# A two-layer decoder trunk on one core: the mixer's fourteen input columns in another order

## The chip, the cores and the metric

The kernel runs on one core of one Trainium2 chip. The metric is the device time of one execution in microseconds (us). A core has five engines with queues of their own: TensorE (PE), VectorE (DVE), ScalarE (ACT), GpSimd (POOL), and SyncE (SP), which here issues most of the DMAs. Each engine works off its own queue in order; the engines wait for each other through semaphores.

## The reference

The input x has 512 positions of 1024 values, in 32-bit floats. Two layers do three residual steps each, of which the middle one is the mixer:

```python
for l in range(DEPTH):                      # DEPTH = 2
    x = x + 0.5 * swiglu(rms_norm(x, norm_ffn1[l]), ffn1...[l])
    h = rms_norm(x, norm_mix[l])
    proj = h @ w_in[l]                      # the columns of three groups of heads
    p_rwkv = token_shift(proj[..., :D_SHIFT], shift_mu[l])   # r, k, v, low rank
    y_rwkv = rwkv7_mixer(p_rwkv, ...)       # 6 heads of 64
    y_attn = dilated_attention(q, k, v)     # 6 heads, three patterns of blocks of 128
    y_conv = conv_mixer(u, ...)             # 256 channels
    x = x + concat(y_rwkv, y_attn, y_conv) @ w_out[l]
    x = x + 0.5 * swiglu(rms_norm(x, norm_ffn2[l]), ffn2...[l])
```

The convolution group takes two halves of its columns, `z = u1 * sigmoid(u2)`, convolves each channel with 31 taps along the positions, normalizes over the 256 channels and applies SiLU. The RWKV group mixes each projected column with that of the position before (token shift), makes decays and rates from the low-rank columns, and runs a recurrence over the positions.

## The kernel before

**Tiling.** x is kept transposed, as eight tiles of 128 channels by 512 positions. Each product of 32-bit floats is made of three matmuls of rounded parts (`mm3`, L124 to L126: high part by high part, high by low, low by high). A weight of 128 x 1024 comes by a DMA of SP into a buffer `raw`; ScalarE copies its high part `hi` (L113) and VectorE makes the low part `lo` (L118); for some of them ScalarE and an adding DMA make it instead (L115, L116). Three buffers of each are turned over; a generator `feed` issues the weights of a stage ahead of their use. PSUM has four banks of tag g, two of b and two of c.

**The norm.** The square sums over the channels are gathered on VectorE while x is finished. `norm_sum` (L201) adds them over the partitions with four small matmuls and takes the root, `norm_spread` (L208) spreads the result over all partitions with four more (L196) and copies it to the tile R. The projected columns are multiplied by R after the matmuls.

**The mixer's columns.** The generator `columns` (L358) makes 14 columns of `w_in`, each of 8 x 3 matmuls, and gives control back after each three. The order of the columns in it is also written into the list of weights (L342). In before it makes the gate and the value of the first convolution pair (12, 10), then the low-rank column (9), three of k (3, 4, 5), three of r (0, 1, 2), three of v (6, 7, 8), and the second convolution pair (13, 11). `finish` (L402) multiplies a column by R and does the token shift; `conv_gate` (L977) makes z of a pair.

**The RWKV preparation.** Between pieces of the columns the program places the preparation for three groups of two heads: `first` (low-rank matmuls, decays, scans), `second` (L478: r into the tile AR), `scores` (L484: matmuls of BK and AR at L491, then copies to XM and masked copies to GG at L497), `fourth` (BF on GpSimd), `third` (the products of v; transposes at L536), `fifth` (transposes at L549). `step(n)` sets n pieces of columns in between, and `need` runs the columns until the named one is there. `inverses` (L565) sends the scores XM through DRAM (dX) into a tile Ei of 96 blocks of 32 x 32, inverts them with 60 operations of VectorE (L584, L590) through a buffer tm, copies the transpose (L593), and sends both back to DRAM, from where `load` brings them as EB.

**The convolution's taps.** `taps` (L994) sets a sum to the last tap on ScalarE and adds the other 30 with one operation of VectorE each (L1007), on 482 to 511 positions. They have a low priority, so that the scheduler may set other work ahead of them, and they may be bound to stand behind a given instruction (`after`). In before, those of the first pair are bound behind `second(2)`, those of the second pair behind the copy that ends the inverse.

**Behind the columns.** The generator `filler` makes the attention's projection (L873 to L875, each output on a PSUM bank of tag g), its scores, weights and values (`att_core`, L907), and the end of the convolution (`conv`, L1012: the mean over the channels by two matmuls at L1017, one for each pair; the squares and their sums at L1026; the spread at L196; the normalized result `chi`, `clo`). The recurrence of eight steps (p3, p4, s1 to s4, L637 to L707) is placed in between by numbers of steps. The product with `w_out` starts with the convolution's results, as soon as they are there.

**What sets the order.** Within an engine, the order follows the order of the program and the priorities; a scheduler writes the queues when the kernel is built. Buffers of the same name are shared: `conv_gate` of the first pair uses the buffers x7 (as "cu") and x6 (as "cw"), and tm in the inverse also uses x7, as do some temporaries of the preparation.

Of the kernel before, what the change touches and what calls it, by code (L numbers as in the profile page):

```python
# [40 lines left out]
NP = 3  # L41
# [41 lines left out]
class Kern:  # L83
# [213 lines left out]
    def mixer(self, l):  # L297
        nc, tc, I = self.nc, self.tc, self.I
# [4 lines left out]
        def pa(n, j=0, w=1):  # L303
            o = l * NPAR + PAR[n] + j
            return self.par[:, o : o + w]

        mx = ctx.enter_context(tc.tile_pool(name=self.n("mix"), bufs=1))
        mt = lambda j, sh, nm, dt=F32: mx.tile(sh, dt, tag=f"m{j}", name=self.n(nm))
# [24 lines left out]
        L = m1.tile([P, T], F32, name=self.n("L"))  # L333
# [5 lines left out]
        pp = tc.tile_pool(name=self.n("prep"), bufs=1)  # L339
        pr = pp.__enter__()  # L340

        srcs = [(I["win"][l, c], 1024) for c in (12, 10, 9, 3, 4, 5, 0, 1, 2, 6, 7, 8, 13, 11)]  # L342
        srcs += [(I["watt"][l, w, kp], 2 * H * HD) for w in (1, 0, 2) for kp in range(4)]
        wo = lambda j, a, b: (I["wout"][l, j, :, a * P : b * P], (b - a) * P)
        srcs += [wo(j, 0, 2) for j in range(NH)] + [wo(j, 2, 5) for j in range(NH)]
# [3 lines left out]
        def column(ps):  # L349
            hi, lo = next(self.fd)  # L350
            for k in range(KT):
                s = slice(k * P, (k + 1) * P)
                self.mm3(ps, hi[:, s], lo[:, s], self.xh[k], self.xl[k], k == 0, k == KT - 1)
                yield 1
# [2 lines left out]

        def columns():  # L358

            pss = [self.psum() for _ in range(2)]  # L360
            for ps in pss:
                yield from column(ps)
            self.norm_sum()
            ps = self.psum()
            yield from column(ps)
            self.norm_spread()
            self.conv_gate(0, mt, pss, zp)
            finish(9, L, ps)
            lora_in()
            for n, q in [("k", q) for q in range(NP)] + [("r", q) for q in range(NP)] + [("v", q) for q in range(NP)]:  # L370
                ps = self.psum()
                yield from column(ps)
                if n == "k":
                    finish(3 + q, ks[q], ps)
                elif n == "r":
                    ks[q] = self.xt(q, "r")
                    finish(q, ks[q], ps)
                else:
                    vs[q] = self.xt((3, 5, 4)[q], "vv")
                    finish(6 + q, vs[q], ps)  # L380
                done.add((n, q))
            pss = [self.psum() for _ in range(2)]
            for ps in pss:
                yield from column(ps)
            self.conv_gate(1, mt, pss, zp)

        def step(n):
            for _ in range(n):
# [2 lines left out]
        def need(*a):  # L391
            while a not in done:
                next(work)

        zp, acc, vs, kns = [], [], [None] * NP, {}
        def lora_in():

            A.activation(L[0:32], L[0:32], AF.Tanh)
            A.activation(L[64:128], L[64:128], AF.Tanh, scale=0.5)
            V.tensor_scalar(L[64:128], L[64:128], 0.5, 0.5, op0=ALU.mult, op1=ALU.add)  # L400

        def finish(c, out, ps):  # L402
            raw = pr.tile([P, T + 1], F32, tag="sraw", name=self.n("sraw"), bufs=2)
            G.memset(raw[:, 0:1], 0.0)
            V.tensor_tensor(raw[:, 1:], ps, self.R, op=ALU.mult)
            t = self.nrm.tile([P, T], F32, tag=("acc", "sq")[c % 2], name=self.n("st"))
            A.activation(t, raw[:, 0:T], AF.Copy, scale=pa("mu", c))
            V.scalar_tensor_tensor(out, raw[:, 1:], der[:, c : c + 1], t, op0=ALU.mult, op1=ALU.add)
# [69 lines left out]
        def second(q):  # L478
            AR, BK, Pm = Q[q]
            need("r", q)  # L480
            r = ks[q]
            return V.tensor_tensor(AR[:, :, 1], v3(r), Pm[:, :, 1:], op=ALU.mult)

        def scores(q):  # L484

            AR, BK = Q[q][:2]
            for c0 in range(0, NC, 4):
                pss = [self.psum("b", 2).rearrange("p (c x t) -> p c x t", c=4, x=2) for _ in range(2)]
                for c in range(4):
                    for h in range(2):  # L490
                        mm(pss[h][:, c], lhsT=BK[half[h], c0 + c, h : h + 2], rhs=AR[half[h], c0 + c], start=True, stop=True)  # L491
                    if c % 2 == 1:
                        step(PS[4])
                for h in range(2):
                    r, o = half[h], half[1 - h]
                    A.copy(XM[r, c0 : c0 + 4, q], pss[h][r])
                    V.tensor_tensor(  # L497
                        GG[q][o, c0 : c0 + 4, h],
                        pss[h][o],
                        mask[o].unsqueeze(1).broadcast_to([HD, 4, 2, HD]),  # L500
                        op=ALU.mult,
                    )

            G.tensor_tensor(
                XM[:, :, q, 0], XM[:, :, q, 0], mask[:, 0].unsqueeze(1).broadcast_to([P, NC, HD]), op=ALU.mult
            )
# [35 lines left out]
        def fifth(q):  # L542

            BF = Q[q]
            for c0 in range(0, NC, 4):
                ps = self.psum("b", 2)
                n = min(4, NC - 1 - c0)
                for c in range(n):
                    nc.tensor.transpose(ps[:, c * P : (c + 1) * P], BF[:, c0 + c].rearrange("p x t -> p (x t)"), ident)  # L549
                A.copy(NKB[:, c0 : c0 + n, q], ps.rearrange("p (c h t) -> p c h t", c=4, h=2)[:, 0:n])  # L550
# [58 lines left out]

        att = at = EB = conv = bp = None  # L610
        work = columns()
        first(0)
        first(1)
# [4 lines left out]
        second(1)  # L618
        scores(1)
        fifth(0)  # L620
        self.taps(0, zp, acc, mt, pa, second(2))
        scores(2)
        after = inverses()
        fourth(1)
# [139 lines left out]
        for c in range(NC):  # L764
            n = c + 1 < NC
# [372 lines left out]
```

## Time and profile before

| | |
|---|---|
| median of 3 runs | 2071.22 us (2067.39 to 2073.70) |
| profiled execution | 2071.77 us |
| its span, first to last instruction | 2069.9 us |
| granted TensorE clock, mean | 0.990 |
| read from HBM | 183.47 MB, 93 GB/s over the span |

One execution was recorded instruction by instruction. A row of the timeline gives the start in us, the duration, the engine, the line, the operation with output and inputs, how many followed each other, and in brackets how long the engine waited before and for whom. A row of the waits gives the waiting engine, tile and line, for whom it waited, then the sum in us, how many, and the mean. A row of the windows gives the stretch, then for PE, PEld (TensorE's weight loads), DVE, ACT and POOL the busy time and count, the granted clock, the DMA engines' share, and their GB/s; where only TensorE is asked for it holds PE alone. A row of a group gives least/median/greatest duration in ns.

### The profile page before, as it was taken

The page shows a single profiled execution, that of the slowest core. Times are in us where ns is not written, and L with a number is a line of the kernel's source. Part 1 is how long each engine was busy: PE and PEld are TensorE (multiplying, and loading weights), DVE is VectorE, ACT ScalarE, POOL GpSimd, SP SyncE. Part 2 cuts the span into 40 slices and gives each one's busy share as a digit, 9 for nine tenths or more (in the row PEclk, how much of TensorE's full clock was granted, in tenths as well). Part 3 has the DMA queues.
Part 4 walks back from the last instruction along what each step waited for, and adds up shares of the span by engine and source line. Part 5 has one row for each costly group of instructions (what it writes and reads, how often), then busy time and mean ns, then how long its engine had stood idle before and what let it go on. Part 6 is the DMA issues. An engine that isn't in the chain of part 4 may idle for free.

```text
span 2069.9 us, 26110 instructions
## 1 busy us (share of the span) xinstructions
PE 2028.1 (98%) x10406; PEld 1652.0 (80%) x10406; DVE 1087.2 (53%) x1539; ACT 770.6 (37%) x1162; POOL 346.4 (17%) x324
## 2 busy tenths in 40 slices
PE   8999999989999999999999999999899999999999
PEld 6888888768877888888888888887687678888887
DVE  5545433389866555443335454324898764554422
ACT  4323222563365432323233232226634653323221
POOL 3101101232411311110111111002323112111100
PEclk9999999989999999999999999999999999999999
DMA  4332334443312433333333333334423134323332
GB/s 169 92 102 92 97 110 124 122 110 87 86 58 72 141 97 93 101 94 98 95 101 92 100 94 97 116 116 124 115 80 105 38 104 119 100 92 102 99 110 66
DMA packets 85609, 207.44 MB, mean 100 GB/s; under 512 B 27056, under 2 KB 32688, under 8 KB 85488
## 3 DMA queue, kind: packets, MB, share of 16 engines
q1 hardware_dynamic: 81312, 191.79, 30.7%
q0 software_dynamic: 3744, 13.63, 3.4%
q8 instruction: 81, 1.33, 0.3%
q10 hardware_dynamic: 432, 0.36, 0.1%
q14 instruction: 40, 0.33, 0.0%
HBM read 183.47 MB, written 8.65 MB: 93 GB/s over the span
## 4 chain that ended last, share of the span: by engine, by line
PE 86%; DVE 8%; ACT 3%; issue 2%; DMA 1%; POOL 1%; SPq 0%; ACTq 0%; POOLq 0%; DVEq 0%
PE psg L124 25%; PE psg L126 25%; PE psg L125 25%; DVE cacc L1007 2%; DVE lo L118 1%; PE psg L921 1%; PE psb L491 1%; PE psc L956 1%; DVE xl L178 1%; PE psg L875 1%; DVE Ei L590 1%; PE psg L873 1%; DMA lo<-raw 1%; DVE tm L584 1%; PE psg L874 1%
## 5 line engine op out<-in xcount | busy, mean ns | idle before, releaser
L113 ACT CAST hi<-raw 128x1024 fp32r<-128x1024 f32 (+3 forms) x368 | 350.8, 953 | 965.2 <-PE psg L125 826.9
L124 PE MATMUL psg<-xh,hi 128*128 128x512 f32 x1632 | 644.2, 395 | 7.1 <-ACT xh L177 7.1
L126 PE MATMUL psg<-xh,lo 128*128 128x512 f32 x1632 | 641.8, 393 | 1.8 <-DMA lo<-raw 1.7
L125 PE MATMUL psg<-xl,hi 128*128 128x512 f32 x1632 | 640.2, 392 | 0.2
L118 DVE TENSOR_TENSOR lo<-raw,hi 128x1024 fp32r<-128x1024 f32 (+4 forms) x342 | 461.3, 1349 | 336.3 <-ACT hi L113 326.9
L124 PEld LDWEIGHTS psg<-xh,hi 128*128 128x128 f32 x1632 | 309.0, 189 | 74.5 <-ACT xh L177 7.1
L126 PEld LDWEIGHTS psg<-xh,lo 128*128 128x128 f32 x1632 | 308.8, 189 | 68.1 <-DMA lo<-raw 2.9
L125 PEld LDWEIGHTS psg<-xl,hi 128*128 128x128 f32 x1632 | 309.0, 189 | 67.3 <-DVE xl L178 2.9
L124 PE MATMUL psg<-ah,hi 128*128 128x512 f32 x704 | 273.9, 389 | 0.0
L125 PE MATMUL psg<-al,hi 128*128 128x512 f32 x704 | 273.9, 389 | 0.0
L126 PE MATMUL psg<-ah,lo 128*128 128x512 f32 x704 | 273.9, 389 | 0.0
L224 POOL TENSOR_TENSOR s<-s,u 128x512 f32<-128x512 f32 x88 | 121.3, 1378 | 801.6 <-ACT hi L113 704.6
L223 DVE TENSOR_TENSOR u<-psg,R 128x512 f32<-128x512 f32 x88 | 60.8, 691 | 265.2 <-PE psg L126 264.9
L126 PEld LDWEIGHTS psg<-ah,lo 128*128 128x128 f32 x704 | 132.2, 188 | 27.5
L125 PEld LDWEIGHTS psg<-al,hi 128*128 128x128 f32 x704 | 132.2, 188 | 27.4
L124 PEld LDWEIGHTS psg<-ah,hi 128*128 128x128 f32 x704 | 132.2, 188 | 27.3
L221 DVE TENSOR_TENSOR g<-psg,R 128x512 f32<-128x512 f32 x88 | 60.8, 691 | 124.6 <-PE psg L126 124.6
L186 POOL TENSOR_TENSOR acc<-acc,sq 128x512 f32<-128x512 f32 x42 | 59.1, 1408 | 377.0 <-ACT sq L185 376.4
L1007 DVE SCALAR_TENSOR_TENSOR cacc<-z,par,cacc 128x482 f32<-128x482 f32 (+14 forms) x120 | 104.6, 872 | 1.7
L129 ACT CAST ah<-s 128x512 fp32r<-128x512 f32 x88 | 54.9, 623 | 122.2 <-POOL s L224 122.2
L130 DVE TENSOR_TENSOR al<-s,ah 128x512 fp32r<-128x512 f32 x88 | 59.8, 680 | 22.8 <-ACT ah L129 22.8
L873 PE MATMUL psg<-hi,xh 128*128 128x384 f32 x192 | 65.8, 346 | 4.7 <-ACT nat L898 4.7
(210 smaller groups left out, 1855.8 us busy)
## 6 DMA issues: line engine op xcount, KB each, us to landing
raw<-in_wgu_dram SPq DMA_DIRECT2D x176, 512.0 KB, 3.5
raw<-in_wd_dram SPq DMA_DIRECT2D x64, 512.0 KB, 3.5
raw<-in_win_dram SPq DMA_DIRECT2D x28, 512.0 KB, 3.6
lo<-raw POOLq DMA_DIRECT2D x26, 512.0 KB, 4.6
raw<-in_wd_dram SPq DMA_DIRECT2D x32, 384.0 KB, 3.2
raw<-in_watt_dram SPq DMA_DIRECT2D x24, 384.0 KB, 3.1
raw<-in_wout_dram SPq DMA_DIRECT2D x28, 192.0 KB, 2.3
xs<-x SPq DMA_DIRECT2D x16, 256.0 KB, 2.0
```

The costliest lines, as they stand in the source:

```text
L113: nc.scalar.copy(hi[:, :cols], raw[:, :cols])
L118: nc.vector.tensor_tensor(lo[:, :cols], raw[:, :cols], hi[:, :cols].bitcast(F32), op=ALU.subtract)
L124: mm(out, lhsT=whi, rhs=xhi, start=first, stop=False)
L125: mm(out, lhsT=whi, rhs=xlo, start=False, stop=False)
L126: mm(out, lhsT=wlo, rhs=xhi, start=False, stop=last)
L130: self.nc.vector.tensor_tensor(lo, src, hi.bitcast(F32), op=ALU.subtract)
L186: nc.gpsimd.tensor_tensor(self.acc, self.acc, sq, op=ALU.add)
L221: nc.vector.tensor_tensor(t[0], p[0], self.R, op=ALU.mult)
L223: nc.vector.tensor_tensor(t[1], p[1], self.R, op=ALU.mult)
L224: nc.gpsimd.tensor_tensor(t[2], t[2], t[1], op=ALU.mult)
L873: mm(o, lhsT=self.xh[kk][:, t], rhs=hi[:, s], start=kk == 0, stop=False)
L1007: nc.vector.scalar_tensor_tensor(a[:, d:], z[:, 0 : T - d], pa("dww", u * CW + j), a[:, d:], op0=ALU.mult, op1=ALU.add)
```

## The change

The columns come in the order low-rank, three of k, three of r, first convolution pair, three of v, second convolution pair. The norm's sums (`norm_sum`) stand behind the first column, which is now the low-rank one; the spread, the low-rank column's finish and its activations stand behind the second one (the first of k). The taps of the first pair are called right behind its gate, inside the generator, and are no longer bound to another instruction; they keep their low priority. Nothing is computed otherwise, and the number of matmuls is the same.

```diff
-        srcs = [(I["win"][l, c], 1024) for c in (12, 10, 9, 3, 4, 5, 0, 1, 2, 6, 7, 8, 13, 11)]
+        srcs = [(I["win"][l, c], 1024) for c in (9, 3, 4, 5, 0, 1, 2, 12, 10, 6, 7, 8, 13, 11)]
...
         def columns():
 
-            pss = [self.psum() for _ in range(2)]
-            for ps in pss:
-                yield from column(ps)
+            low = self.psum()
+            yield from column(low)
             self.norm_sum()
-            ps = self.psum()
-            yield from column(ps)
-            self.norm_spread()
-            self.conv_gate(0, mt, pss, zp)
-            finish(9, L, ps)
-            lora_in()
-            for n, q in [("k", q) for q in range(NP)] + [("r", q) for q in range(NP)] + [("v", q) for q in range(NP)]:
+            for n, q in [(n, q) for n in "krcv" for q in range(NP) if n != "c" or q == 0] + [("c", 1)]:
+                if n == "c":
+                    pss = [self.psum() for _ in range(2)]
+                    for ps in pss:
+                        yield from column(ps)
+                    self.conv_gate(q, mt, pss, zp)
+                    if q == 0:
+                        self.taps(0, zp, acc, mt, pa, None)
+                    continue
                 ps = self.psum()
                 yield from column(ps)
+                if (n, q) == ("k", 0):
+                    self.norm_spread()
+                    finish(9, L, low)
+                    lora_in()
                 if n == "k":
                     finish(3 + q, ks[q], ps)
...
                 done.add((n, q))
-            pss = [self.psum() for _ in range(2)]
-            for ps in pss:
-                yield from column(ps)
-            self.conv_gate(1, mt, pss, zp)
...
         fifth(0)
-        self.taps(0, zp, acc, mt, pa, second(2))
+        second(2)
         scores(2)
```

The changed kernel's lines from here on have a number greater by one than before (the taps are at L1008, GG at L498, the mean at L1018).

VectorE's queue around the scores of group 2 in layer 0, before (GG_2568 and GG_2569 are the masked scores of groups 1 and 2, cacc the sum of the first convolution pair, sraw the first v column):

```order
L482 TENSOR_TENSOR AR_3037<-r_3173,Pm_3070 128x8x64
L497 TENSOR_TENSOR GG_2568<-psb_3139,tab 64x4x128
L510 SCALAR_TENSOR_TENSOR r_3173<-r_3173,par,kn_3109 128x512
L1007 SCALAR_TENSOR_TENSOR cacc_3192<-z_2719,par,cacc_3192 128x482
L1007 SCALAR_TENSOR_TENSOR cacc_3192<-z_2719,par,cacc_3192 128x483
L1007 SCALAR_TENSOR_TENSOR cacc_3192<-z_2719,par,cacc_3192 128x484
L1007 SCALAR_TENSOR_TENSOR cacc_3192<-z_2719,par,cacc_3192 128x485
L497 TENSOR_TENSOR GG_2569<-psb_3224,tab 64x4x128
L497 TENSOR_TENSOR GG_2569<-psb_3225,tab 64x4x128
L405 TENSOR_TENSOR sraw_3354<-psg_3180,R_2712 128x512
```

The same place in the changed kernel:

```order
L483 TENSOR_TENSOR AR_2966<-r_3102,Pm_2999 128x8x64
L498 TENSOR_TENSOR GG_2568<-psb_3068,tab 64x4x128
L511 SCALAR_TENSOR_TENSOR r_3102<-r_3102,par,kn_3038 128x512
L498 TENSOR_TENSOR GG_2569<-psb_3122,tab 64x4x128
L498 TENSOR_TENSOR GG_2569<-psb_3123,tab 64x4x128
L498 TENSOR_TENSOR GG_2569<-psb_3142,tab 64x4x128
L498 TENSOR_TENSOR GG_2569<-psb_3143,tab 64x4x128
L991 SCALAR_TENSOR_TENSOR cw_3283<-psg_3110,R_2680 128x512
L406 TENSOR_TENSOR sraw_3354<-psg_3321,R_2680 128x512
```

The four taps between the scores of groups 1 and 2 are gone; a part of the first pair's gate (cw) now stands between GG and the v column.

VectorE's queue at the end of the inverse in layer 0, before (Et is the transposed inverse, lo a weight of the attention's projection, cacc_3589 the second pair's sum):

```order
L584 TENSOR_TENSOR tm_3272<-Ei_3269 96x30
L590 TENSOR_TENSOR Ei_3269<-Ei_3269,tm_3272 96x30
L593 COPY Et_3270<-Ei_3269 96x1024
L1007 SCALAR_TENSOR_TENSOR cacc_3589<-z_3563,par,cacc_3589 128x482
L118 TENSOR_TENSOR lo_4012<-raw_4010,hi_4011 128x768
L1007 SCALAR_TENSOR_TENSOR cacc_3589<-z_3563,par,cacc_3589 128x483
```

There in the changed kernel (cu, cw and z_3287 are of the first pair, cuw and z_3563 of the second):

```order
L585 TENSOR_TENSOR tm_3170<-Ei_3167 96x30
L591 TENSOR_TENSOR Ei_3167<-Ei_3167,tm_3170 96x30
L594 COPY Et_3168<-Ei_3167 96x1024
L989 TENSOR_TENSOR cu_3282<-psg_3109,R_2680 128x512
L993 SCALAR_TENSOR_TENSOR z_3287<-cu_3282,cw_3283 128x512
L993 SCALAR_TENSOR_TENSOR z_3563<-cuw_3559 128x512
L118 TENSOR_TENSOR lo_3687<-raw_3685,hi_3686 128x768
L1008 SCALAR_TENSOR_TENSOR cacc_3289<-z_3287,par,cacc_3289 128x482
L1008 SCALAR_TENSOR_TENSOR cacc_3589<-z_3563,par,cacc_3589 128x482
```

Both gates end behind the inverse, and the taps of both pairs follow it in turn, where before only those of the second pair did.

TensorE's queue around the convolution's mean in layer 0, before (EB, Z, A and E, SVU belong to the recurrence; pT, vt, pe and qkT to the attention):

```order
L947 MATMUL psg_4602<-tab,pe_4498 128x128 x4
L1017 MATMUL psg_4626<-cacc_3192,onesm 128x512
L1017 MATMUL psg_4626<-cacc_3589,onesm 128x512
L641 MATMUL psb_4608<-EB_3570,XM_2570 64x64 x6
L678 MATMUL psb_4617<-A_802_4589,E_785_4516 64x64 x6
L956 MATMUL psc_4631<-pT_4536,vt_3754 64x128 x2
L956 MATMUL psc_4631<-pT_4601,vt_3754 64x128 x3
L650 MATMUL psb_4634<-EB_3570,Z_4615 64x64 x6
L701 MATMUL psc_4591<-SVU_2572,XM_2570 64x64
L1026 MATMUL psg_4660<-onesm,z_2719 128x1
```

In the changed kernel, around the second of the two matmuls of the mean (the first stands 29 rows ahead):

```order
L660 MATMUL psb_4884<-SVU_2572,GG_2569 64x64 x2
L679 MATMUL psb_4918<-A_870_4891,E_853_4803 64x64 x6
L1018 MATMUL psg_4626<-cacc_3589,onesm 128x512
L667 MATMUL psc_4893<-SVU_2572,GG_2567 64x64 x2
L667 MATMUL psc_4893<-SVU_2572,GG_2568 64x64 x2
L667 MATMUL psc_4893<-SVU_2572,GG_2569 64x64 x2
L702 MATMUL psc_4893<-SVU_2572,XM_2570 64x64
L1027 MATMUL psg_4660<-onesm,z_3287 128x1
L922 MATMUL psg_4673<-qkT_3972,qkT_4338 128x512
```

The second matmul of the mean and the sums of the squares now stand behind the products at L679 of the recurrence's last step; behind them only the last step's products at L667 and L702 are left of the recurrence.

## The prediction

> **What bounds the kernel now.** I read the page's busy times first, then the busy time and clock by stage, the list of what TensorE waited for, the timelines around its longest waits, and the clock in stretches of 4 us.
>
> ```profile
> span 2069.9 us, 26110 instructions
> PE 2028.1 (98%) x10406; PEld 1652.0 (80%) x10406; DVE 1087.2 (53%) x1539; ACT 770.6 (37%) x1162; POOL 346.4 (17%) x324
> ```
>
> TensorE (PE) is busy for 98% of the span. Its matmuls stay the same in number and kind, so the change can only move idle time (42 us in all) and time at a low clock. The next rows cut the mixer of layer 0 at the first column, the first attention matmul, and the first W_out matmul; then the first two stages in layer 1.
>
> ```profile
> 372.40:496.60 124.20, 114.49 (x549) 89.53 (x548) 86.52 (x135) 75.28 (x108) 37.32 (x41) 0.93 0.47 115
> 496.60:602.90 106.30, 102.62 (x975) 85.99 (x973) 87.34 (x203) 47.06 (x104) 34.73 (x37) 0.97 0.29 79
> 602.90:720.00 117.10, 114.82 (x669) 86.45 (x668) 71.15 (x150) 62.59 (x129) 24.69 (x25) 1.00 0.34 97
> ...
> 1401.40:1525.60 124.20, 114.47 (x559) 89.81 (x558) 87.82 (x138) 76.11 (x108) 37.20 (x41) 0.95 0.47 115
> 1525.60:1630.00 104.40, 101.25 (x986) 84.83 (x984) 87.38 (x207) 47.78 (x106) 35.19 (x38) 0.98 0.29 81
> ```
>
> The columns' stage loses 9.7 us of idle time in each layer and 7% and 5% of the clock; the second stage loses 3.7 and 3.2 us of idle time. TensorE's waits over the whole program:
>
> ```profile
> PE psb L491 <- DVE GG L497: 10.6, 4, 4.8
> ...
> PE psb L536 <- DVE vv L408: 5.0, 2, 2.5
> PE psg L873 <- ACT nat L898: 4.7, 6, 1.8
> ...
> PE psb L549 <- ACT SVU L540: 0.4, 2, 0.2
> ```
>
> Two long waits per layer, for GG and for vv, are most of it. TensorE, VectorE and GpSimd there, in layer 0:
>
> ```profile
> 428.75 1.87 PE L491 MATMUL psb<-AR,BK 64*128 64x128 f32 x16 [0.48 <-DVE GG L497]
> ...
> 460.90 2.79 PE L491 MATMUL psb<-AR,BK 64*128 64x128 f32 x16 [4.80 <-DVE GG L497]
> ...
> 479.14 0.66 PE L536 MATMUL psb<-tab,vv 128*128 128x128 f32 x4 [2.48 <-DVE vv L408]
> ```
> ```profile
> 453.06 7.06 DVE L1007 SCALAR_TENSOR_TENSOR cacc<-z,par,cacc 128x482 f32<-128x482 f32 x4
> 460.15 1.41 DVE L497 TENSOR_TENSOR GG<-psb,tab 64x512 f32<-64x512 f32 x2
> ```
> ```profile
> 454.23 4.61 POOL L514 TENSOR_TENSOR BF<-BK,fd 64x1024 f32<-64x1024 f32 x2
> ```
>
> Four taps of the convolution stand in VectorE's queue ahead of GG and take 7.06 us, while GpSimd works on BF; GG starts as they end, and TensorE right after. The wait for vv has the same origin. The clock, in stretches of 4 us (TensorE's busy time, instructions, granted clock):
>
> ```profile
> 436.00:440.00 4.00, 4.00 (x11) 0.50 0.41 130
> ...
> 460.00:464.00 4.00, 3.10 (x17) 0.50 0.66 131
> 464.00:468.00 4.00, 4.00 (x13) 0.75 0.28 49
> ...
> 480.00:484.00 4.00, 4.00 (x16) 0.61 0.62 197
> ...
> 592.00:596.00 4.00, 4.00 (x14) 0.54 0.00 0
> ```
> ```profile
> 1488.00:1492.00 4.00, 3.30 (x17) 0.50 0.68 135
> 1492.00:1496.00 4.00, 4.00 (x17) 0.82 0.33 57
> ...
> 1508.00:1512.00 4.00, 4.00 (x18) 0.69 0.66 197
> ```
>
> Half the clock follows both long waits, and comes twice (436 and 592) in stretches of small matmuls without a long wait.
>
> **The columns' stage.** The changed order has no tap ahead of GG and vv, so 4.80 + 2.48 + 0.2 = **7.5 us** of waiting go in each layer. With them go the two drops of the clock behind: busy time by missing clock is 3.10 x 0.50 + 4.00 x 0.25 + 4.00 x 0.39 = 4.1 in layer 0 and 3.30 x 0.50 + 4.00 x 0.18 + 4.00 x 0.31 = 3.6 in layer 1. The drop at 436 stays, since the scores and low-rank matmuls before it stand as close as before.
>
> What comes in: the same preparation meets fewer column matmuls as cover. A column matmul is issued every 0.227 us:
>
> ```profile
> 372.40 0.39 PE L124 MATMUL psg<-xh,hi 128*128 128x512 f32 x1
> 372.63 0.39 PE L125 MATMUL psg<-xl,hi 128*128 128x512 f32 x1
> ```
>
> The scores of one half wait for GG of the other; nine matmuls between them left 0.48 us (the row at 428.75), so the six that now stand at group 2 leave 0.48 + 3 x 0.227 = 1.2. The low-rank matmuls of group 2 follow the scores by six instead of nine: 0.7. The first low-rank matmul stands 20 instead of 27 matmuls behind the spread of the norm: up to 1.6, less the two convolution products that VectorE no longer does first (1.2): I take 0.6. The vv of two v columns wait behind a weight copy on ScalarE: 0.5 each. The square sums meet 8 instead of 12: 0.2. Together **+3.7**, between 1.5 (only the two derived from 0.48) and 6 (all uncovered). Stage: -7.5 - 4.1 + 3.7 = -7.9 in layer 0, -7.4 in layer 1. The norm's sums, a column earlier, have their last square by then and cost nothing in themselves.
>
> **The bank that is held.** The gate of the first convolution pair shares a buffer with the inverse's tm, so it waits for the whole inverse and keeps one of four PSUM banks; the fourth tile of the attention projection needs that bank. The load of the inverse:
>
> ```profile
> 472.39 1.05 ACT L113 CAST hi<-raw 128x1024 fp32r<-128x1024 f32 x1 [1.14 <-PE psg L125]
> ```
> ```profile
> 480.05 0.34 SPq L579 DMA_DIRECT2D Ei<-dX  x1
> ```
> ```profile
> 486.80 0.18 DVE L584 TENSOR_TENSOR tm<-Ei 96x30 f32<-96x30 f32 x1
> ...
> 525.12 1.13 DVE L593 COPY Et<-Ei 96x1024 f32<-96x1024 f32 x1
> ```
> ```profile
> DMA to landing us min/median/max: 3.3/3.7/4.2
> ```
>
> The load goes 7.7 us after a column's end frees the weight buffer, and lands 3.7 later: 11.4. It now stands two weight loads earlier, behind the end of the second convolution column. The inverse ran 39.4 us with ten taps between (0.74 each): 32 without, less some other rows: 31. So the bank is free 11.4 + 31 + 0.6 = 43.0 us after that column. TensorE needs 5 columns (27.2), some 6.5 for the small matmuls of bv, vv and NKB, and 48 attention matmuls (8.5, at the pitch below): 42.2. Cost **+0.8** per layer, between 0 and 5 (a load that lands at 4.2 behind a late weight).
>
> **The taps behind the inverse.** All 60 now stand there, against 30 before.
>
> ```profile
> L1007 DVE SCALAR_TENSOR_TENSOR cacc<-z,par,cacc x120: 706/734/2265, 453.1 to 1597.4; 128x482 f32<-128x482 f32 x4, 128x483 f32<-128x483 f32 x4, 128x484 f32<-128x484 f32 x4, 128x485 f32<-128x485 f32 x4
> ```
> ```profile
> 497.08 0.35 PE L873 MATMUL psg<-hi,xh 128*128 128x384 f32 x1
> 497.26 0.34 PE L874 MATMUL psg<-lo,xh 128*128 128x384 f32 x1
> ```
>
> VectorE, from the free bank to the last tap: 60 taps of 0.73 are 44, the recurrence, norms and splits between them about 39 by their durations: 83 us. TensorE to the same point: 240 attention matmuls of 0.178 are 43, eight steps of the recurrence of some 3.1 are 25, transposes and first scores 13: 81. The lists match, so VectorE makes TensorE wait: **+2**, between 0 and 10 (taps as slow as all were on average, 0.872 us: 60 x 0.14 more).
>
> **The convolution's chain.** Between the mean and the first W_out matmul:
>
> ```profile
> 585.17 1.88 PE L1017 MATMUL psg<-cacc,onesm 128*128 128x512 f32 x4
> ...
> 596.41 2.08 PE L196 MATMUL psg<-tab,lnt 128*128 128x128 f32 x8
> ...
> 602.95 0.50 PE L124 MATMUL psg<-chi,hi 128*128 128x512 f32 x1
> ```
> ```profile
> 389.67 1.05 PE L196 MATMUL psc<-tab,rnt 128*128 128x128 f32 x8
> ```
>
> From 587.05 to 602.95 it took 15.9 us, with small matmuls at half clock (2.08 against 1.05). The recurrence's last steps, which covered it, now stand ahead of it; about 9 us of TensorE's own work are left. A chain of 13, between 10 (all at full clock, no queue) and 15.9, leaves **+4** idle, and 0.7 for the second gate behind it. In exchange the waits for nat (4.7 us in six, 2.35 per layer) go, since those banks are now given back earlier.
>
> **The sum.** Layer 0: -7.9 + 0.8 + 2 + 4.7 - 2.35 = -2.75; layer 1: -7.4 + 5.15 = -2.25. Together -5.0. The profiled execution took 2071.77 us, 0.55 above the median of 2071.22, so I put **2066.5 us**. 0.3% is about 6.2 us, what a measurement can tell from no change.
>
> **The rule of the clock.** The Trainium skill, "TensorE: Matmul & The Clock Gate", section "What's actually happening", says that the array falls to half clock after an idle window of about 3.4 us. The drop behind the 4.80 us agrees; those at 436 and 592, with TensorE busy, do not. It speaks against the change where the chain leaves TensorE idle, and gives the third rival below.
>
> **The rivals.**
> 1. *Taps late, chain bare (slower).* It decides on VectorE between the inverse and the mean, once that list is some 4 us longer than TensorE's. For it: the mean tap of 0.872, and GpSimd works beside. Against it: those 2.265 us taps ran beside BF, which is now done. Price: +8 for the taps and +3 for a chain of 15.9, in each layer: -5 + 22 = +17, or 2088; with half of it 2077. Chance 0.24.
> 2. *Front won, little given back (faster).* The chain is 10 us, the lists match, half of the 3.7 is covered: -3 - 2 - 1.8 more per layer: -5 - 14 = -19, or 2053. For it: the chain of before held waits in queues. Chance 0.24.
> 3. *Half clock in the bare chain.* The sum takes the clock there as it was. Were the first W_out columns at half clock for some 3.4 us more (as long as the stretch of 480 to 484), 1.7 and a slower L196 (1.05) come in per layer: +5.5, or 2072. Chance 0.12.
> That nothing moves is no rival: the rows of both engines above show the taps gone from the front.
>
> **How the numbers follow.** The sum has 0.40, and its own bounds reach from 2058 to 2073, about half of it below 2065. Faster by over 0.3%: 0.24 + 0.18 = 0.42. Within: 0.20 from the sum, 0.10 from the third rival: 0.30. Slower: 0.24 + 0.04: 0.28. The range, 2051 to 2082, leaves out the ends of the first two rivals.
>
> **What would show it.** Right: no wait of L492 for GG over 1.5 us, none for vv over 1; clock above 0.95 over the columns; first attention matmul about 8 us earlier; a wait of some us before the second L1018 and the first W_out matmul. Wrong: the mean more than 92 us behind the freed bank (first rival), a long wait of the attention projection for cu, or half clock over the columns without waits.

## The result, and the profile after

The changed kernel took 2082.59 us, the median of five runs (2080.71 to 2087.09); the kernel before took 2069.52 us in five runs beside it (2067.39 to 2073.70). The ratio is 1.0066, with a 95% interval of 1.0047 to 1.0085: slower by 13 us, where 2066.5 was forecast. The profiled execution took 2081.91 us. The head of its page:

```profile
span 2080.1 us, 26121 instructions
PE 2039.2 (98%) x10406; PEld 1658.0 (80%) x10406; DVE 1076.6 (52%) x1539; ACT 770.4 (37%) x1162; POOL 345.6 (17%) x324
```

TensorE does the same 10406 matmuls and is busy for 11 us longer. Its waits over the whole program, of which these rows belong to the mixer (sum, how many, longest):

```profile
...
PE psb L689 <- DVE SVU L681: 4.0, 5, 0.9
...
PE psb L679 <- ACT yt L837: 3.1, 2, 1.5
...
PE psb L537 <- DVE vv L409: 1.9, 2, 1.0
...
PE psg L874 <- DVE cu L989: 1.2, 2, 0.6
...
PE psb L492 <- DVE GG L498: 0.5, 2, 0.3
```

The long waits of before are gone (GG 10.6 to 0.5, vv 5.0 to 1.9); in their place stand many small ones in the recurrence and in the group norm behind it. The stages by windows: the columns, and then all from the first attention matmul to the first matmul of the next feed-forward part, in layer 0 and in layer 1 (TensorE's busy time, instructions, granted clock). First the second of these stages in the kernel before, since the prediction cut it otherwise:

```profile
496.55:678.42 181.87, 176.98 (x1458) 0.98 0.27 77
1524.16:1703.74 179.58, 175.21 (x1457) 0.99 0.27 78
```

And both stages in the changed kernel:

```profile
372.61:489.17 116.56, 112.41 (x549) 0.97 0.51 122
489.17:683.14 193.97, 183.61 (x1457) 0.92 0.25 72
1405.92:1520.64 114.72, 110.81 (x548) 0.99 0.51 124
1520.64:1714.84 194.20, 183.80 (x1458) 0.92 0.25 72
```

The columns are 7.6 us shorter in layer 0 (124.2 before) and 7.7 in layer 1 (122.4 before). The rest of the mixer is 12.1 us longer in layer 0 and 14.6 in layer 1, at a clock of 0.92. Where that clock comes from, in steps of 3.41 us in layer 0:

```profile
580.76:584.17 3.41, 3.28 (x60) 1.00 0.00 0
584.17:587.59 3.42, 2.01 (x49) 1.00 0.03 5
587.59:591.00 3.41, 2.65 (x27) 0.50 0.00 0
...
601.24:604.65 3.41, 3.41 (x14) 0.50 0.00 0
...
614.89:618.30 3.41, 3.41 (x12) 0.50 0.00 0
618.30:621.72 3.42, 3.42 (x18) 1.00 0.00 0
```

From 587.59 to 618.30 the clock is 0.50 without a break: 30.7 us, nine such steps, against 6.8 us (592.33 to 599.15) before. In layer 1 the changed kernel is at half clock behind the columns for as long in all, in three stretches of 6.8, 20.5 and 3.4 us. TensorE is busy for most of the time. What it does there:

```profile
583.86 0.52 PE L667 MATMUL psc<-SVU,GG 128*64 128x64 f32 x9
584.31 0.56 PE L642 MATMUL psb<-EB,XM 64*64 64x64 f32 x12
584.71 0.52 PE L679 MATMUL psb<-A,E 64*64 64x64 f32 x12
585.69 0.33 PE L702 MATMUL psc<-SVU,XM 64*64 64x64 f32 x2 [0.47 <-ACT SVU L680]
...
587.39 0.78 PE L689 MATMUL psb<-SVU,NKB 128*64 128x64 f32 x12 [0.95 <-DVE SVU L681]
588.10 0.90 PE L702 MATMUL psc<-SVU,XM 64*64 64x64 f32 x10
...
593.51 0.90 PE L679 MATMUL psb<-A,E 64*64 64x64 f32 x12 [0.47 <-ACT A L662]
594.35 2.07 PE L1018 MATMUL psg<-cacc,onesm 128*128 128x512 f32 x2
```
```profile
600.70 3.15 PE L1027 MATMUL psg<-onesm,z 128*128 128x1 f32 x14
...
613.21 0.80 PE L124 MATMUL psg<-chi,hi 128*128 128x512 f32 x1
```

Up to the mean the recurrence's last steps and the group norm's matmuls run here without any large matmul between them: most fill 64 x 64 or 128 x 64 of the array, with waits between them for the copies of the step before. Then come the second matmul of the mean, the sums with one column each, some matmuls of the attention, what is left of the last step (L667 and L702), and at 613.21 the first W_out matmul, 18.9 us behind the start of the mean. Before, about one and a half steps of the recurrence stood in that stretch, and more than one behind the first W_out matmul; now only the end of the last step is left.

### The profile page after: what moved, and what is told of

Same layout as the page of the kernel before. It is cut to its first block, busy times and chain, and to the rows that moved or that the text cites. A ratio compares the mean times of both kernels' runs of the same rounds, so it can differ in the third digit from the quotient of the medians.

```text
span 2080.1 us, 26121 instructions
## 1 busy us (share of the span) xinstructions
PE 2039.2 (98%) x10406; PEld 1658.0 (80%) x10406; DVE 1076.6 (52%) x1539; ACT 770.4 (37%) x1162; POOL 345.6 (17%) x324
## 4 chain that ended last, share of the span: by engine, by line
PE 83%; DVE 10%; ACT 3%; issue 2%; DMA 2%; POOL 1%; SPq 0%; DVEq 0%; ACTq 0%; POOLq 0%
PE psg L124 25%; PE psg L125 25%; PE psg L126 25%; DVE cacc L1008 3%; DVE lo L118 1%; PE psg L922 1%; DVE tm L585 1%; DVE Ei L591 1%; PE psc L957 1%; PE psb L492 1%; DMA lo<-raw 1%; PE psg L948 1%; DVE xl L178 1%; PE psg L874 0%; POOL gst L191 0%
## 5 line engine op out<-in xcount | busy, mean ns | idle before, releaser
L124 PEld LDWEIGHTS psg<-ah,hi 128*128 128x128 f32 x704 | 132.2, 188 | 27.3
L186 POOL TENSOR_TENSOR acc<-acc,sq 128x512 f32<-128x512 f32 x42 | 59.1, 1408 | 379.3 <-ACT sq L185 378.6
L1008 DVE SCALAR_TENSOR_TENSOR cacc<-z,par,cacc 128x483 f32<-128x483 f32 (+18 forms) x120 | 89.3, 776 | 0.4
```

The source lines that it names most:

```text
L124: mm(out, lhsT=whi, rhs=xhi, start=first, stop=False)
L186: nc.gpsimd.tensor_tensor(self.acc, self.acc, sq, op=ALU.add)
L1008: nc.vector.scalar_tensor_tensor(a[:, d:], z[:, 0 : T - d], pa("dww", u * CW + j), a[:, d:], op0=ALU.mult, op1=ALU.add)
```

## The experiments

Each was timed beside the kernel before (2069 to 2070 us in each set). Theory 1: the taps' place does it. All 60 stand behind the inverse, so the convolution's chain comes behind the recurrence, and there TensorE goes to half clock because its matmuls fill little of the array.

**Only the taps moved.** The columns and the norm of before:

```diff
-        self.taps(0, zp, acc, mt, pa, second(2))
+        second(2)
...
+            self.taps(0, zp, acc, mt, pa, after)
             self.taps(1, zp, acc, mt, pa, after)
```

> The order of before, columns and norm as before; only the taps of the first pair are moved behind the inverse. Theory 1 (all of the loss comes from the taps' place: with 60 of them behind the inverse the convolution's chain comes after the recurrence, where matmuls that fill little of the array leave TensorE at half clock): the front wins GG, vv and the clock behind them, 11 us in each layer, the back loses 12 to 14 us as in the changed kernel, so 2069 to 2080, with a stretch of over 15 us at clock 0.50 before the first W_out matmul. Theory 2 (the changed column order itself costs it: the bank held by the first pair, fewer covering columns): the back stays as before, no such stretch, 2044 to 2055.

Measured: 2080.68 us, ratio 1.0051 (1.0035 to 1.0068). Its two stages in layer 0:

```profile
372.60:485.01 112.41, 110.06 (x548) 0.98 0.53 126
485.01:684.19 199.18, 186.86 (x1458) 0.91 0.24 70
```

The columns win 11.7 us and the rest loses 17.3. So the taps' place alone, in the old order of columns, gives the time that the changed kernel has; theory 2 falls. The time is 0.7 us over the range that theory 1 gave. The columns' stage is 4.1 us shorter than in the changed kernel (2.3 in layer 1): so much the new order costs there. The prediction had 3.7 us of idle time for it; of the 4.1, 1.8 are idle time (116.56 - 112.41 against 112.41 - 110.06), of the 2.3, 1.6.

**The inverse's buffer apart.** The changed kernel, where the first gate no longer waits for the inverse:

```diff
-            tm = self.xt(7, "tm")[0 : 4 * nb]
+            tm = pr.tile([P, 256], F32, name=self.n("tm"))[0 : 4 * nb]
```

> The changed kernel, with the inverse's buffer tm in a tile of its own, so that the first gate and its taps need not wait for the inverse. Theory 1: the chain comes while the recurrence still runs, the half clock behind 580 us goes to some 7 us as in before, and most of the front's gain stays: 2050 to 2064, below both kernels. Theory 2 and a theory 3 (VectorE has too much to do in all from the inverse to the mean, wherever the taps begin): the chain is as late, 2078 to 2086.

Measured: 2064.50 us, ratio 0.9978 (0.9968 to 0.9987), half a microsecond over the range. Its stages in layer 0 and in layer 1, and its chain in layer 0:

```profile
372.47:488.99 116.52, 110.69 (x549) 0.99 0.50 121
488.99:671.67 182.68, 175.02 (x1458) 0.98 0.26 77
1394.76:1512.82 118.06, 112.28 (x549) 0.97 0.50 120
1512.82:1698.82 186.00, 178.25 (x1458) 0.96 0.26 75
```
```profile
593.82 0.56 PE L642 MATMUL psb<-EB,XM 64*64 64x64 f32 x12
...
596.25 0.50 PE L124 MATMUL psg<-chi,hi 128*128 128x512 f32 x1
...
597.10 0.56 PE L679 MATMUL psb<-A,E 64*64 64x64 f32 x12
```

In layer 0 the gain of the columns stays and nearly all of the loss behind goes: W_out begins at 596.25, with more than one step of the recurrence still to come. In layer 1 the run keeps less: the columns are 4.3 us shorter than before (7.7 in the changed kernel), and the rest is 6.4 longer (186.00 against 179.58; 14.6 in the changed kernel). Why the layers differ was not followed. One shared buffer made the change slower: without it the time is 18 us less. It also rules out theory 3.

**The taps behind GG, in the order of before.**

```diff
-        self.taps(0, zp, acc, mt, pa, second(2))
-        scores(2)
+        second(2)
+        self.taps(0, zp, acc, mt, pa, scores(2))   # scores now returns its last GG
```

> The kernel before, its columns and norm untouched; the first pair's taps are bound behind the last masked scores of group 2 instead of behind second(2), still ahead of the inverse. Theory 1: the wait for GG (4.8 us) and the clock's drop behind it (1.5 + 1.0) go in each layer, the wait for vv stays, and the chain stays under the recurrence: 2050 to 2062. Theory 5 (what is won in the front is lost behind, whatever the taps do): 2066 to 2076.

Measured: 2062.20 us, ratio 0.9962 (0.9950 to 0.9974), a little over the range and faster than both kernels. Its waits and its stages in layer 0:

```profile
...
PE psb L537 <- DVE vv L408: 6.6, 2, 3.3
...
PE psb L491 <- DVE GG L497: 0.9, 2, 0.5
```
```profile
372.28:489.04 116.76, 110.88 (x549) 0.97 0.50 122
489.04:671.07 182.03, 176.30 (x1458) 0.98 0.27 77
```

GG's wait is nearly gone, vv's stays (6.6 us, 5.0 before), and the rest of the mixer keeps the 181.9 us of before in layer 0; in layer 1 it takes 182.5 against 179.6. Theory 5 falls. This and the run before it can't be told apart by their intervals, so no gain of the new column order itself shows.

**Added matmuls.** Results that nobody reads, to fill the array in the bare stretch. The first form put two of 192 columns behind L679 in the steps from 5 on, one of 256 behind L689 in the steps from 4 on, and two of 384 behind the sums:

```diff
+            if c >= 5:
+                for i in range(2):
+                    mm(ps[:, 256:448], lhsT=ident, rhs=B["A1"].rearrange("p q x -> p (q x)"), start=True, stop=True)
...
+        for u in range(2):
+            mm(ps[:, 128:512], lhsT=self.tb("ident"), rhs=zp[u][:, 0:384], start=True, stop=True)
```

> The changed kernel with added matmuls whose results nobody reads, 128 x 128 by 192 to 384 columns, in the last recurrence steps and the convolution's end: 2688 columns in each layer, 4.5 us at full clock by the 0.85 us that the mean's 512 columns take. Theory 1: the array is filled enough to stay at or come back to full clock, so the added work makes it faster: 2066 to 2077. Theory 4 (the stretch is a chain of dependent steps that lasts as long at any clock): the added work comes on top, 2086 to 2094.

> As the run with added matmuls on 128 x 128, in the same order of instructions, but each on 64 x 64 of the array: as long, and a quarter of the array filled. Theory 1, if what counts is how much of the array works: the half clock stays and the added work costs up to double, 2088 to 2102. If what counts is only that TensorE is not idle (the rule of an idle window in the Trainium skill, page TensorE: Matmul & The Clock Gate, section What's actually happening): as the full tiles do.

Measured: 2065.08 us with 128 x 128 (ratio 0.9981, 0.9971 to 0.9991) and 2070.24 with 64 x 64 (1.0002, 0.9987 to 1.0017). More work made the changed kernel 17 us faster, but against the changed kernel these two do not prove the clock: with the added matmuls the scheduler moved the chain's sums ahead of the recurrence's last step, and W_out's first columns ahead of most of it. Against each other they do bear on it: they have one order, but for neighbours on TensorE that change places, and with a quarter of the array filled the kernel takes 5.2 us more (ten executions of each, 2062.46 to 2068.40 and 2065.75 to 2076.49). Four more runs were made to keep the chain where the changed kernel has it. The first kept the additions at 8 columns:

> The changed kernel with the added matmuls cut to 8 columns each, which leaves the order of the chain as it was there: the mean behind the recurrence's last step. Theory 1 (the array's filling and the order count, not the mere number of instructions): the half clock stays, 2079 to 2087. If small additions are enough to hold the clock: below 2075.

Measured: 2084.97 us, ratio 1.0075 (1.0058 to 1.0092), as the changed kernel. The second added 1408 columns (one of 192 behind L679 and one of 256 behind L689 from step 6 on, two of 384):

> The changed kernel with fewer added matmuls on 128 x 128 (1408 columns in each layer, 2.4 us at full clock), so that the convolution's sums still stand behind the recurrence's last products as in the changed kernel. If the filling itself lifts the clock (theory 1): half clock for under 15 us in each layer and 2066 to 2077. If the gain of the run with 2688 columns came only from its other order, in which the chain starts ahead of the recurrence's last step: the half clock stays, and the added work costs 2.4 to 4.8 us in each layer, 2086 to 2093.

Measured: 2080.95 us, ratio 1.0055 (1.0039 to 1.0072), between the two cases and inconclusive: the filling returned about what it cost, and the mean had moved ahead of the last step's L679 and L667. The last pair has the 2688 columns of the first form and nearly the order of the changed kernel (two of 192 behind L679 from step 5 on, four of 384 behind the sums), once on 128 x 128 and once on 64 x 64:

> The changed kernel with added matmuls on 128 x 128 of the array, 2688 columns in each layer (4.5 us at full clock), as many as in the first such run, but placed so that the convolution's mean and sums stand behind the recurrence's last step, as in the changed kernel itself. Theory 1 (half clock is most of the loss behind the attention's projection, and filling the array lifts it): 2066 to 2077. Theory 6 (the first such run gained only by its order, the chain ahead of the recurrence's last step): the chain is bare as before and the added work comes on top, 2086 to 2098.

> The same order and the same added columns, each on 64 x 64 of the array. If the clock goes by how much of the array works: more time at 0.50 than the run on 128 x 128, and 3 us or more slower than it. If it goes by TensorE being occupied at all: the same as that run, within 2 us.

Measured: 2083.00 us (1.0064, 1.0041 to 1.0087) and 2089.49 us (1.0086, 1.0064 to 1.0108). The six executions of each overlap (2078.21 to 2088.90 and 2084.96 to 2091.65), and the profiles are of the fastest of the first kernel and the slowest of the second, so the rows show the two further apart than they usually are. The added matmuls behind the sums (now L1032) are eight instructions; first in the run on 128 x 128, with the clock in the steps around them:

```profile
600.30 4.35 PE L1032 MATMUL psg<-z,tab 128*128 128x384 f32 x8
```
```profile
596.57:599.98 3.41, 3.41 (x31) 1.00 0.00 0
599.98:603.39 3.41, 3.41 (x8) 0.50 0.00 0
603.39:606.81 3.42, 3.12 (x13) 1.00 0.00 0
```

Then in the run on 64 x 64:

```profile
603.33 5.38 PE L1032 MATMUL psg<-z,tab 64*64 64x384 f32 x8
```
```profile
605.27:608.68 3.41, 3.41 (x7) 0.50 0.00 0
608.68:612.09 3.41, 3.41 (x10) 0.50 0.00 0
```

The step from 599.98 in the first and the step from 605.27 in the second are busy throughout. On the full array one such step brings the clock back in the next; on a quarter of it the clock stays at 0.50. In layer 1 it is the same: the clock is back after one step of L1032 on the full array, and still low behind a step filled by L1032 on the quarter. So in these steps the array's filling decides, not TensorE's idle time. With it goes the time of two kernels that differ in nothing else but neighbours changing places: the medians lie 6.5 us apart, in the same direction as the 5.2 us of the first pair. The full array does not always hold the clock: over the first kernel's six executions the mean granted clock was 0.984 to 0.991, and the one with the lowest clock was the slowest.

The absolute range of theory 1 (2066 to 2077) was missed, and that of theory 6 (2086 to 2098) too: four of the added matmuls stand on the chain itself, since the root behind the sums waits for them, 4.35 us here, and the filled kernel ends even with the changed one (2082.59). The clock thus paid back about the added work, by estimate some 5 us in each layer (4.5 us at full clock); it is not the whole loss. The other part is the order: the first form, with as many columns but the chain ahead of the last step, is 17.9 us faster than this one, and some of that is again clock. How the loss divides between the two was not settled.

**The projection drawn out.**

```diff
-HOP = (1, 1, 2)
+HOP = (1, 1, 1)
```

> The changed kernel with HOP (1, 1, 1) instead of (1, 1, 2): three pieces of the attention's projection in each recurrence step instead of four, so that its large matmuls last one step longer. Theory 1: one step fewer runs at half clock, 2070 to 2080. If the chain of the convolution alone sets the time: 2080 to 2086.

Measured: 2084.23 us, ratio 1.0063 (1.0044 to 1.0081). In layer 0 the last large matmul of the projection starts at 574.6 instead of 566.5, but the mean still stands behind the recurrence's last step and the clock is low for 23.9 us around it (20.5 and 3.4), with another 6.8 us at 548.9. The time lies in the range of the chain alone (2080 to 2086), and theory 1's number was wrong: large matmuls ahead of the stretch did not help it here.

## Why the prediction was wrong

The columns' stage was right in total and in its mechanism. Forecast were -7.9 and -7.4 us; measured were -7.6 and -7.7. The first attention matmul came 7.4 us earlier, GG waits 0.3 us and vv 1.0 us at most, and the clock over the columns is 0.97 and 0.99. By parts, the total is partly luck. The stage before, cut at the same matmuls (in layer 1 the prediction cut it 1.4 us too late):

```profile
372.40:496.55 124.15, 114.44 (x548) 0.93 0.47 115
1401.78:1524.16 122.38, 112.65 (x548) 0.94 0.47 116
```

Idle time fell by 5.6 and 5.8 us, where -7.5 + 3.7 = -3.8 was forecast; busy time fell by 2.0 and 1.8, where the clock was to give 4.1 and 3.6. The covering columns cost less than the forecast, and the half clock behind the waits had cost less than its missing half.

Behind the columns the clock was wrong. The terms forecast there (0.8 for the bank, 2 for the taps, 4.7 for the chain, -2.35 for nat) make +5.15 of idle time in each layer, and no low clock. TensorE's idle time in that stage went from 181.87 - 176.98 = 4.9 to 193.97 - 183.61 = 10.4 us in layer 0, +5.5, and from 4.4 to 10.4 in layer 1, +6.0. Its busy time, with the same matmuls, went up by 183.61 - 176.98 = 6.6 us in layer 0 and by 183.80 - 175.21 = 8.6 in layer 1. The two parts make the whole growth of 12.1 and 14.6 us, and the busy part alone, 15.2 us, is nearly as large as the 16.1 us by which the forecast was off.

The step that failed is the sentence under the third rival, "The sum takes the clock there as it was", which put the clock behind the columns at nothing. Half clock took 30.7 us instead of 6.8 in layer 0:

```profile
587.59:618.30 30.71, 28.06 (x144) 0.50 0.06 18
```

Half of the busy time there would be 14.0 us, against 3.4 before; the 6.6 us that came in are less. In part that is because thin matmuls lose less than half: the twelve of L679 took 0.52 us at clock 1.00 and 0.90 at 0.50. The rest was not followed. In layer 1 half clock took 30.7 us instead of 3.4, so in both layers a microsecond more of it came with some 0.3 us more of busy time (6.6 for 23.9, 8.6 for 27.3).

That the idle time agrees (5.5 and 6.0 for 5.15) is luck too. The bank held TensorE for 0.6 us in each layer (forecast 0.8), and the waits for nat went as forecast. But the chain was to leave 4 us idle between the mean and the first W_out matmul. That stretch in layer 0, before and after:

```profile
587.05:602.95 15.90, 15.20 (x154) 0.79 0.11 34
```
```profile
596.42:613.21 16.79, 15.37 (x71) 0.50 0.10 31
```

The chain took 16.8 us, not 13, and longer than the prediction's upper 15.9; and only 1.4 of it are idle, against 0.7 before, because TensorE works through it at half clock. The other idle time came ahead of the mean (some 8 us there, 3 before), where the bare recurrence waits for its own copies (L689, L679, L651). The prediction's own bounds also did not follow from its terms: with the taps and the chain at their upper ends the sum is 2066.5 + 2 x (8 + 2.9) = 2088, not 2073.

The third rival had the mechanism, with a price of 2.75 us in each layer and a chance of 0.12. It was priced as one stretch of 3.4 us. The rows to price it rightly stood in the prediction: half clock at 436 and 592, "in stretches of small matmuls without a long wait". The change made the second of these stretches long and bare, so it had to be priced by its length.

The first rival's mark was met, with its mechanism only in part. The mean began 95.9 us behind the freed bank (498.47 to 594.35), where the mark was 92; the last tap ended 0.9 us ahead of it, 95.0 behind the bank, where the forecast was 83. The rival's price, 2077 to 2088, lies around the measured time, but most of it (8 of 11 us in each layer) was for slow taps, and they were not slow. VectorE in that time:

```profile
498.47:593.45 94.98, 87.61 (x947) 74.33 (x947) 85.20 (x178) 43.64 (x103) 37.37 (x39) 0.97 0.28 76
```
```profile
DVE yb L821 <- POOL gst L191: 5.2, 3, 2.9
```

It was busy for 85.2 us, the third column, close to the list of 83, and idle for 9.8, of which 5.2 were waits for GpSimd's root in the group norm, with taps queued behind them. The list was right; that the queue stops in it was left out. A tap took 44.66 / 60 = 0.74 us, not the 0.872 that this rival stood on.

The chain's cover was named in the prediction and priced as idle time alone (4.7). The runs show that it is worth more: where W_out begins under the recurrence, as in the kernel before and with the inverse's buffer apart, the clock of that stage in layer 0 is 0.98 and not 0.92.

## What to carry to other kernels

Work that is thin on the array (64 x 64 tiles, one column at a time) should not be left alone on TensorE, even when it keeps it busy: price a bare stretch by its length at half clock, not by its waits (here some 0.3 us for each us of it). When low-priority work is moved out of one engine's way, look where the work that depends on it lands in TensorE's order; binding the taps behind one more instruction won 7.5 us, moving them behind the inverse lost 11. And look for shared buffers: here one small temporary held 30 taps behind an inverse with which they had nothing to do.

## What the runs showed of the hardware

The clock changed between 1.00 and 0.50 only, on a grid of 3.41 us: it was low for nine steps in layer 0, and single steps in the run on 128 x 128 went 1.00, 0.50, 1.00. The Trainium skill, "TensorE: Matmul & The Clock Gate", section "What's actually happening", gives a free-running window of 3413 ns, and the trace agrees. By the same section of the Trainium skill the half clock comes after an idle window. The traces show that it also comes without one. This is the kernel before:

```profile
588.91:592.33 3.42, 3.42 (x45) 1.00 0.02 5
592.33:595.74 3.41, 3.41 (x11) 0.50 0.00 0
```

A window that was busy throughout, most of it with small matmuls, was followed by half clock. Nor was a busy window enough to leave it, as the run on 64 x 64 shows (605.27 to 608.68). At which filling the clock falls and rises was not settled: the steps around those shown have mixtures of shapes.
